# A Hymba decoder layer on one core: Silu gates, biases asked for a head ahead, memory tiles in the last group, value weights split between output products, and the cross norm in the exponential

## The chip, the cores and the metric

The kernel runs on one core of a Trainium2 chip, as one program in one launch. The metric is the device time of one execution in microseconds (us). The median of the runs is given, and beside it one execution recorded by the hardware profiler. TensorE (PE) multiplies; VectorE (DVE), ScalarE (ACT) and GpSimd (POOL) work on tiles in on-chip memory (SBUF) and in the accumulators (PSUM). SyncE (SP) asks for most transfers from device memory; ACT and POOL have queues of their own for a few.

## The reference

One layer with 512 tokens of width 1024: a half-weighted feed-forward, a mixer in which a state-space part (SSD, 16 heads in 4 groups) and 8 differential-attention heads share input and output projections, cross-attention into 256 memory tokens with 4 heads, and a second feed-forward. Cut to what the change touches:

```python
def swiglu(h, w_in, w_out):
    gate, up = jnp.split(h @ w_in, 2, axis=-1)
    return (jax.nn.silu(gate) * up) @ w_out

# differential attention: logits = q @ k * scale + bias[head], softmax, w = p0 - lam * p1

def memory_cross_attention(h, mem_n, w_cq, w_ck, w_cv, w_co):
    q = (h @ w_cq).reshape(bsz, seqlen, CROSS_HEADS, CROSS_HEAD_DIM)
    k = (mem_n @ w_ck).reshape(bsz, mlen, CROSS_HEADS, CROSS_HEAD_DIM)
    v = (mem_n @ w_cv).reshape(bsz, mlen, CROSS_HEADS, CROSS_HEAD_DIM)
    logits = jnp.einsum('bqhd,bkhd->bhqk', q, k) * (CROSS_HEAD_DIM ** -0.5)
    p = jax.nn.softmax(logits, axis=-1)
    ...

x = x + 0.5 * swiglu(rms_norm(x, norm_ffn1_w), ...)
x = x + hybrid_mixer(rms_norm(x, norm_mix_w), ...)
x = x + memory_cross_attention(rms_norm(x, norm_cross_w), rms_norm(mem, norm_mem_w), ...)
x = x + 0.5 * swiglu(rms_norm(x, norm_ffn2_w), ...)
```

## The kernel before

**Tiles and products.** Activations lie transposed: eight tiles `x[0..7]` of 128 channels x 512 tokens. Each float32 number is split into a high and a low half of the type that PE multiplies fast (`split_into`, line 152: ACT copies the high half, DVE subtracts it for the low one), and a product is three matmuls: high by high, high by low, low by high (`mm3`, line 312). A weight is loaded by SP into a raw buffer `wr` (six of them) and split into `wh` and `wl` (three of each; `load_w`, line 172), so a split waits until PE is done with the weight three before it. `proj` (line 318) runs over the eight input tiles: 24 matmuls of 128x512. The feed-forwards use larger Strassen-like blocks, `quad` (line 257), whose accumulators are called `qa`, `qb` and `qe`.

**Stages.** First feed-forward (0 to 358 us), memory keys and the norm of the mixer (to 384), attention heads and SSD groups (to 792), memory values (to 823), output product of the SSD part (to 868), cross-attention and its output product (to 987), second feed-forward and final norm.

**What sets the order.** `Order` (line 57) runs a list of dense generators one after another: `queries_keys`, `values`, `group_dense`, `out_attn`, `memory_values`, `out_proj` (added from line 1033 on). Each `yield` lets chains run that were spawned with `od.spawn(generator, after)`; a chain's step is due when the modelled time of the matmuls issued so far, `od.t`, has passed it. What a step issues enters the program there. The compiler's scheduler then orders PE, ACT and DVE; SP and POOL stay in program order. All engines work in order, so an instruction that waits holds up what stands behind it.

**The places of the change.** A gate of the feed-forward is `silu(g) * u`. `gated` (line 415) and `ffn_quads` (line 425) compute it as `tanh(g/2)` on ACT and `(tanh + 1) * g` on DVE, twice the Silu, which later factors take back. `queries_keys` (line 678) makes the queries `pq` and keys `pk` of a head and asks on ACT's queue for its tile `bias` of relative positions; `head` (line 689) adds the bias to the scores on DVE, exponentiates on ACT, and transposes the weights on PE (`pt`). In the SSD part `group_dense` (line 807) makes, for each group, two tiles by `xbc_tile` (line 794: a product `pxbc`, a convolution `conv` with one ACT and three DVE instructions that read its PSUM bank, and a Silu by `silu2`), two more of them, and two products `pz`. `group` (line 830) is a chain: transposes `pxt` and `pbt`, states `st`, decay rows `gate` and `th` that ACT's queue fetches from `cum_d`, then `y`, its square `ysq` on ACT, a sum on POOL, the matmul `pn`, and a row by two matmuls `nrow` (`row_of`, line 360). `out_attn` (line 773) is the attention's share of the output product (`pm`). Its last call, for outputs 5 to 7, loads its three weights at the start and spawns `memory_prep`: eight memory tiles `mem` through SP and eight splits `hm` on ACT and DVE. `memory_values` (line 985) multiplies the memory with eight weights `wcv` into four banks `pcv`. `Stat.finish` (line 388) makes a norm: eight `nps` matmuls over the sum of squares `nacc`, a small column by POOL, then two `nrow` matmuls and a copy for the row. `cross_dense` (line 1056) multiplies the queries of the cross-attention with this row; `cross` (line 1067) takes their scores and exponentials.

Of the kernel before, what the change touches and what calls it, by code (L numbers as in the profile page):

```python
# [14 lines left out]
ALU = mybir.AluOpType  # L15
# [85 lines left out]
def body(tc, a, dbg=None):  # L101
# [313 lines left out]
    def gated(pg, pu, row):  # L415
        gate = s2("gate")
        V.tensor_tensor(gate, pg, row, ALU.mult)
        th = s2("th")
        S.activation(th, gate, AF.Tanh, scale=0.5)
        V.scalar_tensor_tensor(gate, th, 1.0, gate, ALU.add, ALU.mult)  # L420
        if pu is not None:
            V.tensor_tensor(gate, pu, gate, ALU.mult)
        return gate

    def ffn_quads(xs, wq, st, nq, made, places, sums=None, fresh=False):

        for q in range(nq):
            for out in quad(xs, next(wq), next(sums) if sums else None, fresh and q == 0):
                if out is None:
                    yield  # L430
            gs, us = out
            gate, th = s4("gate"), s4("th")
            for i in range(2):
                row = st.row[:, None, i * H : (i + 1) * H].to_broadcast([P, 2, H])
                V.tensor_tensor(gate[:, 2 * i : 2 * i + 2], halves(gs[i]), row, ALU.mult)
            S.activation(th, gate, AF.Tanh, scale=0.5)
            V.scalar_tensor_tensor(gate, th, 1.0, gate, ALU.add, ALU.mult)
            for i in range(2):
                V.tensor_tensor(th[:, places[i]], halves(us[i]), gate[:, 2 * i : 2 * i + 2], ALU.mult)
            made(th)  # L440
            yield
# [42 lines left out]
    def ffn1(h, wa, on_final, at_out):  # L484
        row4, xs = None, []
        wq, plain = iter(a["f1q"]), a["f1i"]
        for ti, (_, nf) in enumerate(THIRDS):
            g = []
            nq = nf // 2
            if ti == 0:  # L490
# [6 lines left out]
                V.tensor_scalar(row4, st1.row, 0.25, None, ALU.mult)  # L497
# [179 lines left out]

    def queries_keys(hd):
        pq = acc("pq")
        yield from proj(pq, load_w(a["wq"][hd]), h)  # L680
        q = split("q", pq, -1.0)
        bias = s2("bias")
        S.dma_start(bias, bass.AP(rel_z.tensor, rel_z.offset + hd * P * (RW + 1) + P - 1, [[RW, P], [1, T]]))
        pk = acc("pk")
        yield from proj(pk, load_w(a["wk"][hd]), h)
        kq = split("k", pk)
        od.spawn(head(hd, q, kq, bias), W["h0"])
# [84 lines left out]

    def out_attn(hg, o0, o1, prep=False):
        if prep:
            od.spawn(memory_prep(hm2, 1.5), 4.0)
# [3 lines left out]
        for o in range(o0, o1):  # L779
            po = acc("pm")  # L780
            yield from proj(po, ws.get(o) or load_w(a["woa"][hg, o], 4 * P), heads)
            V.tensor_tensor(x[o], x[o], po, ALU.add)
        if o1 == KT:
            ya[4 * hg : 4 * hg + 4] = [None] * 4
# [22 lines left out]
    def group_dense(g):  # L807
        bc, xs, zs = [], [], []
        yield from xbc_tile(8 + g, bc)
# [175 lines left out]
    def memory_values():  # L985
# [5 lines left out]
        for k in range(KT - 2):  # L991
            w = load_w(a["wcv"][k])
# [31 lines left out]
    def upd_c(o, po):  # L1024
# [4 lines left out]
        if o == KT - 1:  # L1029
            h.clear()  # L1030
            od.spawn(st_c.finish(), 3.0)
# [24 lines left out]
    def cross_dense(hd):  # L1056
# [3 lines left out]
        q = []  # L1060
        for j in range(2):
            qf = s2("cqf")
            V.tensor_tensor(qf, ps[j], st_c.row, ALU.mult)
            q.append(split("cq", qf, 0.0625))
        od.spawn(cross(hd, q), W["c0"])

    def cross(hd, q):
        pth = [None, None]
        es = [None, None]
        for s in range(3):  # L1070
            if s < 2:
# [6 lines left out]
                V.tensor_reduce(mx, ps, axis=AX.X, op=ALU.max, negate=True)  # L1078
                sm = small("csm", 2)
                e = es[s] = s2("ce", shape=(P, 2, MEM))  # L1080
                for i in range(2):
                    S.activation(e[:, i], ps[:, i], AF.Exp, bias=mx[:, i : i + 1], accum_out=sm[:, i : i + 1])
# [184 lines left out]
    def ffn2():  # L1267
# [28 lines left out]
        for c, (_, nf) in enumerate(THIRDS2):  # L1296
            g = []
            yield from ffn_quads(xs_2, wq, st_2, nf // 2, block_tiles(g, nf // 2), BY_BLOCK, in_sums, c == 0)
            if c == 0:
                col4 = small("col4", 4, bufs=1)  # L1300
                ncol4 = small("ncol4", 4, bufs=1)
                V.tensor_scalar(col4, st_2.col, 0.25, None, ALU.mult)
                V.tensor_scalar(ncol4, st_2.col, -0.25, None, ALU.mult)
# [100 lines left out]
```

## Time and profile before

| | us |
|---|---|
| median of three runs (lowest to highest) | 1330.35 (1329.05 to 1330.5) |
| the profiled execution | 1330.79 |
| its span in the trace | 1329.0 |

The span is the time from the first to the last instruction in the trace; the rest of the profiled execution's time, 1.79 us, lies around it. A page of the profile gives each engine's busy time. A list of waits gives, for an engine, how long it stood idle before instructions of a kind and which instruction ended that. The chain of waits follows the last instruction back to what released it. A row of the timeline gives start and duration, engine, line, operation, output and inputs, and in brackets the idle time before it. In a group's row the numbers after the bar are the busy time in us, the mean in ns of one instruction, and the idle time of the engine before them.

### The profile page before, as it was taken

How to read it: one execution, taken by the hardware profiler on the slowest of the kernel's cores; microseconds unless marked ns; L12 is line 12 of the kernel's file. 1: busy time of each engine (PE TensorE's matmuls, PEld its weight loads, DVE VectorE, ACT ScalarE, POOL GpSimd, SP SyncE). 2: the span in 40 equal slices, each digit the busy share in tenths (PEclk: the TensorE clock that was granted, in tenths of full speed). 3: DMA queues.
4: the chain of work that ended last, by engine and by line, in shares of the span. 5: the costliest groups of instructions: out<-in, count | busy, mean ns of one | idle time of the engine just before them, and what ended most of it. 6: DMA issues, size and time to landing. Idle time of an engine off the chain costs nothing.

```text
span 1329.0 us, 20041 instructions
## 1 busy us (share of the span) xinstructions
PE 1307.0 (98%) x7769; PEld 1137.9 (86%) x7769; DVE 974.2 (73%) x1527; ACT 663.7 (50%) x1114; POOL 113.4 (9%) x127
## 2 busy tenths in 40 slices
PE   9999999999999999999999989999999999999997
PEld 7898998899887778777788878888889999989995
DVE  6874778487886486557867786656678878887886
ACT  6442445154454465336644655434465545554564
POOL 0000010000010111010112021020001100000001
PEclk9999999999999999999999999999999999999998
DMA  7335577555573724683365576775138975655662
GB/s 271 111 127 126 128 199 242 137 144 174 190 241 92 196 63 109 185 243 95 88 174 163 126 199 244 195 180 153 64 111 235 250 223 173 194 193 172 191 202 95
DMA packets 74143, 222.71 MB, mean 168 GB/s; under 512 B 8424, under 2 KB 20176, under 8 KB 73696
## 3 DMA queue, kind: packets, MB, share of 16 engines
q1 hardware_dynamic: 52400, 174.42, 38.3%
q0 software_dynamic: 11904, 40.45, 16.4%
q10 hardware_dynamic: 9744, 6.56, 2.4%
q8 instruction: 61, 1.00, 0.3%
q14 instruction: 34, 0.28, 0.1%
HBM read 219.24 MB, written 50.91 MB: 203 GB/s over the span
## 4 chain that ended last, share of the span: by engine, by line
PE 93%; DVE 2%; DMA 1%; ACT 1%; issue 1%; POOL 0%; POOLq 0%; SPq 0%; ACTq 0%; DVEq 0%
PE qb L240 12%; PE po L146 10%; PE pm L146 10%; PE qe L240 8%; PE qa L240 8%; PE pxbc L146 7%; PE pcq L146 3%; PE pz L146 3%; PE pv L146 3%; PE pq L146 3%; PE ob L1189 3%; PE pk L146 3%; PE oa L1189 2%; PE oe L1189 2%; PE pcv L146 2%; PE pa L146 2%
## 5 line engine op out<-in xcount | busy, mean ns | idle before, releaser
L155 ACT ACTIVATE wh<-wr 128x1024 fp32r<-128x1024 f32 (+2 forms) x311 | 316.9, 1021 | 366.7 <-PE po L146 61.8
L156 DVE TENSOR_TENSOR wl<-wr,wh 128x1024 fp32r<-128x1024 f32 (+2 forms) x311 | 365.5, 1177 | 110.4 <-ACT wh L155 108.2
L146 PE MATMUL po<-gh,wh 128*128 128x512 f32 x176 | 68.8, 392 | 0.0
L146 PE MATMUL po<-gl,wh 128*128 128x512 f32 x176 | 68.5, 390 | 0.0
L146 PE MATMUL po<-gh,wl 128*128 128x512 f32 x176 | 68.4, 389 | 0.0
L240 PE MATMUL qa<-hml,wh 128*128 128x256 f32 x216 | 61.1, 283 | 0.0
L240 PE MATMUL qa<-hmh,wl 128*128 128x256 f32 x216 | 61.1, 283 | 0.0
L240 PE MATMUL qa<-hmh,wh 128*128 128x256 f32 x216 | 61.1, 283 | 0.0
L146 PE MATMUL pxbc<-hnh,wh 128*128 128x512 f32 x128 | 52.2, 408 | 0.0
L705 ACT ACTIVATE ec<-ec,mn 128x512 f32<-128x512 f32 (+3 forms) x64 | 35.4, 555 | 32.4 <-DVE mn L704 32.4
L146 PE MATMUL pxbc<-hnh,wl 128*128 128x512 f32 x128 | 50.3, 393 | 0.0
L146 PE MATMUL pxbc<-hnl,wh 128*128 128x512 f32 x128 | 50.2, 392 | 0.0
L511 DVE TENSOR_TENSOR upd<-po,row 128x512 f32<-128x512 f32 x24 | 16.6, 690 | 39.2 <-PE po L146 39.0
L240 PE MATMUL qe<-s31h,wl 128*128 128x256 f32 x152 | 43.2, 284 | 0.5 <-DVE wl L156 0.5
L240 PE MATMUL qb<-s24h,wl 128*128 128x256 f32 x152 | 43.1, 284 | 0.5 <-DVE wl L156 0.5
L240 PE MATMUL qb<-s31h,wh 128*128 128x256 f32 x152 | 43.2, 284 | 0.0
L240 PE MATMUL qe<-s31h,wh 128*128 128x256 f32 x152 | 43.1, 284 | 0.0
L240 PE MATMUL qe<-s24h,wh 128*128 128x256 f32 x152 | 43.0, 283 | 0.0
L240 PE MATMUL qb<-hmh,wh 128*128 128x256 f32 x152 | 43.0, 283 | 0.0
L240 PE MATMUL qe<-s24h,wl 128*128 128x256 f32 x152 | 43.0, 283 | 0.0
L240 PE MATMUL qb<-hmh,wl 128*128 128x256 f32 x152 | 43.0, 283 | 0.0
L240 PE MATMUL qb<-hml,wh 128*128 128x256 f32 x152 | 43.0, 283 | 0.0
(443 smaller groups left out, 4064.6 us busy)
## 6 DMA issues: line engine op xcount, KB each, us to landing
wr<-in_f2q SPq DMA_DIRECT2D x44, 512.0 KB, 4.3
wr<-in_f1q SPq DMA_DIRECT2D x40, 512.0 KB, 4.0
isum<-in_f2q SPq DMA_DIRECT2D x22, 512.0 KB, 5.6
wr<-isum SPq DMA_DIRECT2D x22, 512.0 KB, 4.2
wsum<-in_f2b SPq DMA_DIRECT2D x20, 512.0 KB, 6.5
wr<-wsum SPq DMA_DIRECT2D x20, 512.0 KB, 4.6
wr<-in_f1q POOLq DMA_DIRECT2D x16, 512.0 KB, 6.3
wr<-in_f1o SPq DMA_DIRECT2D x16, 512.0 KB, 4.0
```

The source lines that it names most:

```text
L146: newest_mm[:] = [nc.tensor.matmul(out, w, x, start=start, stop=stop).ins]
L155: S.activation(hi, src, AF.Copy),
L156: V.tensor_tensor(lo, src, hi.bitcast(F32), ALU.subtract),
L240: newest_mm[:] = [nc.tensor.matmul(out, a_[:, wc], b_, start=first and f == 0 and kp == 0 and j == 0, stop=kp == n - 1 and j == 2, skip_gr ...
L511: V.tensor_tensor(upd, po, row4, ALU.mult)
L705: S.activation(ec[:, :n], ec[:, :n], AF.Exp, bias=mn, scale=-1.0, accum_out=sm[c][:, i : i + 1])
L1189: newest_mm[:] = [nc.tensor.matmul(ps, a_[:, ts], b_[:, ws], start=first and k == 0 and j == 0, stop=k == n - 1 and j == 2, skip_group_che ...
```

## The change

It has five parts. (1) The feed-forwards' gates become one ACT instruction, `Silu`, in place of `Tanh` and a DVE product, and factors of 0.25 become 0.5; an ACT_TABLE_LOAD is added ahead of the first Silu, of the first head's exponential and of the second feed-forward's first Silu. (2) `queries_keys` asks for the bias of the next head before its own products (the first one for its own too). (3) `memory_prep` is spawned at the start of the last `group_dense`, with its splits 3.0 apart in place of 1.5, and so its eight transfers stand on SP's queue behind the first weight of that group and ahead of all its others. (4) Two of the three last output products are each followed by the load and split of one value weight, and `memory_values` takes these two. (5) The norm ahead of the cross-attention stops after its column: the queries are split straight from PSUM, and the column scales the maximum and the exponential.

```diff
@@ -415,11 +415,8 @@
     def gated(pg, pu, row):
         gate = s2("gate")
         V.tensor_tensor(gate, pg, row, ALU.mult)
-        th = s2("th")
-        S.activation(th, gate, AF.Tanh, scale=0.5)
-        V.scalar_tensor_tensor(gate, th, 1.0, gate, ALU.add, ALU.mult)
-        if pu is not None:
-            V.tensor_tensor(gate, pu, gate, ALU.mult)
+        S.activation(gate, gate, AF.Silu)
+        V.tensor_tensor(gate, pu, gate, ALU.mult)
         return gate
 
     def ffn_quads(xs, wq, st, nq, made, places, sums=None, fresh=False):
@@ -433,8 +430,7 @@
             for i in range(2):
                 row = st.row[:, None, i * H : (i + 1) * H].to_broadcast([P, 2, H])
                 V.tensor_tensor(gate[:, 2 * i : 2 * i + 2], halves(gs[i]), row, ALU.mult)
-            S.activation(th, gate, AF.Tanh, scale=0.5)
-            V.scalar_tensor_tensor(gate, th, 1.0, gate, ALU.add, ALU.mult)
+            S.activation(gate, gate, AF.Silu)
             for i in range(2):
                 V.tensor_tensor(th[:, places[i]], halves(us[i]), gate[:, 2 * i : 2 * i + 2], ALU.mult)
             made(th)
@@ -494,7 +490,7 @@
                     else:
                         g.append(split("g", gated(*made, st1.row)))
                 row4 = s2("row4")
-                V.tensor_scalar(row4, st1.row, 0.25, None, ALU.mult)
+                V.tensor_scalar(row4, st1.row, 0.5, None, ALU.mult)
                 for n in range(NPLAIN - 2):
                     xs.append(block_sums(2 * n, C_FFN1, of_halves(h[2 * n], h[2 * n + 1])))
                     pg, pu = acc("pg"), acc("pu")
@@ -675,16 +671,24 @@
                 yield
         vs[hg] = [split("v", pv[tb]) for tb in range(4)]
 
+    biases = {}
+
+    def ask_bias(hd):
+        biases[hd] = s2("bias")
+        S.dma_start(biases[hd], bass.AP(rel_z.tensor, rel_z.offset + hd * P * (RW + 1) + P - 1, [[RW, P], [1, T]]))
+
     def queries_keys(hd):
+        if hd == 0:
+            ask_bias(0)
+        if hd < 7:
+            ask_bias(hd + 1)
         pq = acc("pq")
         yield from proj(pq, load_w(a["wq"][hd]), h)
         q = split("q", pq, -1.0)
-        bias = s2("bias")
-        S.dma_start(bias, bass.AP(rel_z.tensor, rel_z.offset + hd * P * (RW + 1) + P - 1, [[RW, P], [1, T]]))
         pk = acc("pk")
         yield from proj(pk, load_w(a["wk"][hd]), h)
         kq = split("k", pk)
-        od.spawn(head(hd, q, kq, bias), W["h0"])
+        od.spawn(head(hd, q, kq, biases.pop(hd)), W["h0"])
 
     def head(hd, q, kq, bias):
         es, w0, w1 = {}, {}, {}
@@ -770,9 +774,9 @@
         ya[hd] = split("ya", pt, wsub)
         dump(f"ya_{hd}", ya[hd][0])
 
+    wcv = []
+
     def out_attn(hg, o0, o1, prep=False):
-        if prep:
-            od.spawn(memory_prep(hm2, 1.5), 4.0)
         ws = {o: load_w(a["woa"][hg, o], 4 * P) for o in range(o0, o1) if prep}
         yield lambda: all(y is not None for y in ya[4 * hg : 4 * hg + 4])
         heads = ya[4 * hg : 4 * hg + 4]
@@ -780,6 +784,8 @@
             po = acc("pm")
             yield from proj(po, ws.get(o) or load_w(a["woa"][hg, o], 4 * P), heads)
             V.tensor_tensor(x[o], x[o], po, ALU.add)
+            if prep and len(wcv) < 2:
+                wcv.append(load_w(a["wcv"][len(wcv)]))
         if o1 == KT:
             ya[4 * hg : 4 * hg + 4] = [None] * 4
 
@@ -806,6 +812,8 @@
 
     def group_dense(g):
         bc, xs, zs = [], [], []
+        if g == 3:
+            od.spawn(memory_prep(hm2, 3.0), 1.0)
         yield from xbc_tile(8 + g, bc)
         yield from xbc_tile(12 + g, bc)
         for j in range(2):
@@ -989,7 +997,7 @@
 
         banks = [(tb, n) for tb in range(2) for n in range(2)]
         for k in range(KT - 2):
-            w = load_w(a["wcv"][k])
+            w = wcv[k] if k < len(wcv) else load_w(a["wcv"][k])
             for tb, n in banks:
                 part(k, w, tb, n)
                 yield
@@ -1028,7 +1036,7 @@
         dump(f"x2_{o}", x[o])
         if o == KT - 1:
             h.clear()
-            od.spawn(st_c.finish(), 3.0)
+            od.spawn(islice(st_c.finish(), 1), 3.0)
 
     hm, hm2 = [], []
     od.add(memory_keys())
@@ -1057,11 +1065,7 @@
         ps = [acc("pcq") for _ in range(2)]
         for j in range(2):
             yield from proj(ps[j], load_w(a["wcq"][2 * hd + j]), h_c)
-        q = []
-        for j in range(2):
-            qf = s2("cqf")
-            V.tensor_tensor(qf, ps[j], st_c.row, ALU.mult)
-            q.append(split("cq", qf, 0.0625))
+        q = [split("cq", ps[j], 0.0625) for j in range(2)]
         od.spawn(cross(hd, q), W["c0"])
 
     def cross(hd, q):
@@ -1076,10 +1080,12 @@
                         mm3(ps[:, i], q[j], ck[2 * hd + j], j == 0, j == 1, wc=qs)
                 mx = small("cmx", 2)
                 V.tensor_reduce(mx, ps, axis=AX.X, op=ALU.max, negate=True)
+                col = st_c.col[:, 2 * s : 2 * s + 2]
+                V.tensor_tensor(mx, mx, col, ALU.mult)
                 sm = small("csm", 2)
                 e = es[s] = s2("ce", shape=(P, 2, MEM))
                 for i in range(2):
-                    S.activation(e[:, i], ps[:, i], AF.Exp, bias=mx[:, i : i + 1], accum_out=sm[:, i : i + 1])
+                    S.activation(e[:, i], ps[:, i], AF.Exp, bias=mx[:, i : i + 1], scale=col[:, i : i + 1], accum_out=sm[:, i : i + 1])
                 rc = small("crc", 2)
                 V.reciprocal(rc, sm)
                 for i in range(2):
@@ -1299,8 +1305,8 @@
             if c == 0:
                 col4 = small("col4", 4, bufs=1)
                 ncol4 = small("ncol4", 4, bufs=1)
-                V.tensor_scalar(col4, st_2.col, 0.25, None, ALU.mult)
-                V.tensor_scalar(ncol4, st_2.col, -0.25, None, ALU.mult)
+                V.tensor_scalar(col4, st_2.col, 0.5, None, ALU.mult)
+                V.tensor_scalar(ncol4, st_2.col, -0.5, None, ALU.mult)
             at_end = c == len(THIRDS2) - 1
             if at_end:
                 for n in range(2):
```

Three places show how this moves instructions. The first is on ScalarE (ACT) around the last group's second `pxbc` product; `conv` reads the first product, and the `wh` behind it is the weight of the second. Before, in the last group (`wh_1529_7515` is the second product's weight):

```order
L799 ACTIVATE conv_1482_7313<-pxbc_1474_7270,par_77 128x512
L155 ACTIVATE wh_1515_7445<-wr_1514_7443 128x1024
L790 ACTIVATE th2_1483_7318<-conv_1482_7313 128x512
L155 ACTIVATE wh_1529_7515<-wr_1528_7513 128x1024
L155 ACTIVATE ysh_1493_7355<-y_1448_7101 128x512
L155 ACTIVATE ysh_1495_7360<-y_1463_7193 128x512
```

And of the change (`wh_1533_7517` is the second product's weight, `pxbc_1507_7422` the first product):

```order
L901 ACTIVATE gate_1441_7077<-gate_1441_7077,cum_240 128x128 x3
L159 ACTIVATE hm_1528_7494<-mem_1512_7437,par_77 128x256
L902 ACTIVATE gate_1441_7077<-gate_1441_7077 128x512
L805 ACTIVATE conv_1529_7506<-pxbc_1507_7422,par_77 128x512
L155 ACTIVATE wh_1533_7517<-wr_1532_7515 128x1024
```

The split of the second product's weight stood far ahead of the first product's end; now it stands behind the memory tiles' splits and behind the `conv` that reads that end. On TensorE of the change nothing stands between the two products:

```order
L146 MATMUL pxbc_1507_7422<-hnh_633_3850,wh_1509_7425 128x512
L146 MATMUL pxbc_1507_7422<-hnl_634_3851,wh_1509_7425 128x512
L146 MATMUL pxbc_1507_7422<-hnh_633_3850,wl_1510_7426 128x512
L146 MATMUL pxbc_1531_7514<-hnh_599_3680,wh_1533_7517 128x512
L146 MATMUL pxbc_1531_7514<-hnl_600_3681,wh_1533_7517 128x512
L146 MATMUL pxbc_1531_7514<-hnh_599_3680,wl_1534_7518 128x512
```

The second product's first matmul follows the first product's last, and its third needs `wl`.

The second place is on ACT in the last group's `pz` products, where the second group's `y` is squared (`ysq`). Before (the first 128x512 `wh` here is the first weight of the output products, `wh_1586_7819` the third):

```order
L921 ACTIVATE ysq_1551_7673<-y_1539_7584 128x512
L155 ACTIVATE wh_1580_7807<-wr_1579_7805 128x512
L921 ACTIVATE ysq_1552_7676<-y_1550_7669 128x512
L799 ACTIVATE conv_1553_7685<-pxbc_1544_7627,par_77 128x512
L155 ACTIVATE wh_1583_7813<-wr_1582_7811 128x512
L790 ACTIVATE th2_1554_7690<-conv_1553_7685 128x512
L790 ACTIVATE th2_1559_7725<-pz_1555_7693 128x512
L861 ACTIVATE btk_1577_7797<-pbt_1576_7793 128x384
L155 ACTIVATE wh_1586_7819<-wr_1585_7817 128x512
```

And of the change (`wh_1596_7839` is the third weight of the output products, `wh_1604_7868` the first value weight):

```order
L159 ACTIVATE hm_1556_7664<-mem_1517_7447,par_77 128x256
L929 ACTIVATE ysq_1560_7690<-y_1545_7592 128x512
L155 ACTIVATE wh_1596_7839<-wr_1595_7837 128x512
L929 ACTIVATE ysq_1561_7693<-y_1559_7686 128x512
L159 ACTIVATE hm_1562_7696<-mem_1518_7449,par_77 128x256
L805 ACTIVATE conv_1563_7705<-pxbc_1552_7641,par_77 128x512
L155 ACTIVATE wh_1604_7868<-wr_1603_7866 128x1024
```

The third weight, which takes the buffer of the last `pz` product's weight, moved from behind `conv` to between the two squares.

The third place is on VectorE (DVE) at the end of the first feed-forward, where the last output tiles are added and their squares summed in `nacc`. Before:

```order
L511 TENSOR_TENSOR upd_581_3594<-po_577_3569,row4_77_421 128x512
L512 TENSOR_TENSOR x7_107<-x7_107,upd_581_3594 128x512
L156 TENSOR_TENSOR wl_596_3674<-wr_594_3671,wh_595_3673 128x1024
L386 TENSOR_TENSOR nacc_534_3363<-nacc_534_3363,nsq_582_3597 128x512
L355 TENSOR_SCALAR nv_591_3648<-nps_590_3643 128x4
```

And of the change:

```order
L507 TENSOR_TENSOR upd_569_3543<-po_565_3518,row4_75_417 128x512
L156 TENSOR_TENSOR wl_583_3614<-wr_581_3611,wh_582_3613 128x1024
L508 TENSOR_TENSOR x6_103<-x6_103,upd_569_3543 128x512
L386 TENSOR_TENSOR nacc_528_3343<-nacc_528_3343,nsq_570_3546 128x512
L507 TENSOR_TENSOR upd_575_3574<-po_571_3549,row4_75_417 128x512
L508 TENSOR_TENSOR x7_107<-x7_107,upd_575_3574 128x512
L156 TENSOR_TENSOR wl_590_3654<-wr_588_3651,wh_589_3653 128x1024
L386 TENSOR_TENSOR nacc_528_3343<-nacc_528_3343,nsq_576_3577 128x512
```

In the tiles before the last one, a weight's low half `wl` moved from behind `x` to ahead of it; in the last tile the order is the same.

## The prediction

> **What bounds the kernel now.** I read three views in this order: the head of the page with its chain of waits, the list of what TensorE (PE) waits for, and the same span cut into windows.
>
> ```profile
> span 1329.0 us, 20041 instructions
> PE 1307.0 (98%) x7769; PEld 1137.9 (86%) x7769; DVE 974.2 (73%) x1527; ACT 663.7 (50%) x1114; POOL 113.4 (9%) x127
> PE 93%; DVE 2%; DMA 1%; ACT 1%; issue 1%; POOL 0%; POOLq 0%; SPq 0%; ACTq 0%; DVEq 0%
> ```
>
> PE is busy for 1307.0 of 1329.0 us and is 93% of the chain, so an edit counts only where it removes PE work, removes a PE wait, or makes a new one. Work taken from VectorE (DVE, 73%) or ScalarE (ACT, 50%) is worth nothing by itself.
>
> ```profile
> PE pcv L146 <- ACT wh L155: 3.8, 1, 3.8
> PE pt L150 <- DVE mn L704: 2.6, 1, 2.6
> PE qb L240 <- DVE wl L156: 0.5, 1, 0.5
> PE qe L240 <- DVE wl L156: 0.5, 1, 0.5
> ```
>
> In this list of waits (total, times, longest) two single waits stand out, and the change touches both. Each costs more than its idle time, as two pairs of windows show (columns: length, busy time and count of PE, weight loads, DVE, ACT, POOL, then the granted clock).
>
> ```profile
> 454.63:458.04 3.41, 0.79 (x4) 0.70 (x5) 3.05 (x9) 2.49 (x7) 0.00 (x0) 1.00 0.51 141
> 458.04:461.45 3.41, 3.41 (x10) 2.64 (x9) 2.73 (x10) 1.94 (x8) 0.00 (x0) 0.50 0.63 202
> 792.55:795.96 3.41, 0.15 (x1) 0.15 (x2) 2.94 (x7) 3.41 (x8) 0.00 (x0) 1.00 0.99 258
> 795.96:799.37 3.41, 3.26 (x8) 2.06 (x8) 3.41 (x5) 2.49 (x4) 0.00 (x0) 0.50 0.97 317
> ```
>
> A slice of 3.41 us in which PE was busy for 0.79 or 0.15 us is followed by one at clock 0.50. Half speed over 3.41 us loses 3.41/2 = 1.71 us of PE work. So a wait that empties most of one slice costs itself plus 1.71.
>
> **Biases a head ahead: -4.35.**
>
> ```profile
> 436.37 16.13 DMA bias<-rel_z
> L683 ACTq DMA_DIRECT2D bias<-rel_z x8: 326/338/355, 390.0 to 631.8; - x8
> 457.25 0.33 PE L150 MATMUL pt<-ident,ec 128*128 128x128 f32 x1 [2.64 <-DVE mn L704]
> ```
>
> The wait list blames DVE, but the chain of waits goes on to a bias transfer that took 16.13 us from its issue at 436.37; DVE's score rows were late behind it, and the transposes `pt` behind these. The eight biases are asked for from 390.0 to 631.8, 241.8/7 = 34.5 us apart; asked for one head earlier, the same transfer would land in the middle of the previous head's work. I take the whole wait and its slow slice: 2.64 + 1.71 = 4.35. If the transfer is as slow and lands late in its new place, nothing is gained.
>
> **Memory values: -5.90.**
>
> ```profile
> 794.71 1.04 ACT L155 ACTIVATE wh<-wr 128x1024 fp32r<-128x1024 f32 x1
> 795.81 1.11 PE L146 MATMUL pcv<-wh,hm 128*128 128x512 f32 x2 [3.79 <-ACT wh L155]
> 797.07 0.79 PE L146 MATMUL pcv<-wl,hm 128*128 128x512 f32 x1
> L156 DVE TENSOR_TENSOR wl<-wr,wh 128x1024 fp32r<-128x1024 f32 x280 | 342.3, 1224 | 104.8 <-ACT wh L155 103.4
> ```
>
> PE stands for 3.79 us before the first `pcv`, because the split of its weight starts on ACT only at 794.71. Two half-clock matmuls of about 0.43 us from 795.81 end at about 796.67, and the next starts at 797.07: 0.40 more, for the low half `wl`. With two value weights split between the last output products, PE should find both halves ready: 3.79 + 0.40 + 1.71 = 5.90. What takes the stall's place is below: the eight memory tiles now stand in the third group's work.
>
> **The third group's weight: +3.4, and +0.85 for the clock.** In the order before, ACT splits the weight of the group's second `pxbc` product ahead of `ysh`, long before it is needed:
>
> ```profile
> 732.66 1.06 ACT L155 ACTIVATE wh<-wr 128x1024 fp32r<-128x1024 f32 x1 [0.34 <-PE pz L146]
> 690.00:785.00 95.00, 95.00 (x498) 79.06 (x497) 72.09 (x111) 47.93 (x87) 14.94 (x14) 1.00 0.53 141
> L799 ACT ACTIVATE conv<-pxbc,par 128x512 f32<-128x512 f32 x16 | 12.2, 764 | 0.3 <-PE pxbc L146 0.3
> L802 DVE SCALAR_TENSOR_TENSOR conv<-pxbc,par,conv 128x511 f32<-128x511 f32 x16 | 11.9, 746 | 2.5 <-ACT conv L799 2.5
> 748.71 0.39 PE L146 MATMUL pxbc<-hnh,wl 128*128 128x512 f32 x1
> 748.93 0.39 PE L146 MATMUL pxbc<-hnh,wh 128*128 128x512 f32 x1
> ```
>
> PE has no idle time from 690 to 785. In the changed order that split stands on ACT behind a `conv` that reads the end of the first product, while PE goes straight on to the second. Matmuls start 0.23 us apart (748.71 to 748.93) but end after 0.39, so PE waits (0.39 - 0.23) + 0.76 + 1.06 = 2.0. Two matmuls later it needs `wl`, which DVE makes behind two taps of the convolution: 0.76 + 2 x 0.75 + 1.22 from the product's end, against 0.76 + 1.06 + 2 x 0.23: 1.2 more. The order alone thus gives 3.2; if ACT is late with the gate chain that stands ahead of `conv`, up to 4.1. I take 3.4, nearer the lower end since ACT is busy for 47.93 of 95 us there. The stall is cut by two matmuls of 0.45 us together, so a slice of 3.41 us can be as empty as 0.79 or not, by where its edge falls: 0 or 1.71, and I take half, 0.85.
>
> **The memory tiles, and y of the second group: +3.0.** Eight transfers and eight splits move 30 us ahead:
>
> ```profile
> 711.51 0.93 ACTq L827 DMA_DIRECT2D th<-cum_d  x2
> th<-cum_d ACTq DMA_DIRECT2D x8, 256.0 KB, 16.0
> SPq L946 <- DMA gate<-cum_d: 21.1, 2, 18.2
> 743.51 36.65 SPq L946 DMA_DIRECT2D mem<-in_memT  x8
> L159 ACT ACTIVATE hm<-mem,par 128x256 fp32r<-128x256 f32 x16 | 7.4, 494 | 0.0
> L160 DVE SCALAR_TENSOR_TENSOR hm<-mem,par,hm 128x256 fp32r<-128x256 f32 x16 | 7.2, 477 | 0.2 <-ACT hm L159 0.2
> L155 ACT ACTIVATE wh<-wr 128x512 fp32r<-128x512 f32 x23 | 14.4, 628 | 12.7 <-PE pm L146 4.6 <-PE oa L1189 1.9 <-PE qb L240 1.8
> L921 ACT ACTIVATE ysq<-y 128x512 f32<-128x512 f32 x8 | 5.0, 622 | 6.8 <-PE pm L146 4.8 <-DVE y L919 2.0
> L923 POOL TENSOR_TENSOR ysq<-ysq,ysq 128x512 f32<-128x512 f32 x4 | 6.6, 1662 | 153.4 <-ACT ysq L921 153.4
> 778.09 0.95 PE L146 MATMUL pn<-ones,ysq 128*128 128x1 f32 x8
> ```
>
> On SP's queue the eight issues took 36.65 us, because they wait for the decay rows `gate` and `th` that ACT's queue fetches (21.1 us of waits). Behind them stood value weights; now the weights of the second `pxbc` product and of all that follows in the group do. The rows they then wait for are those of the second group, the last asked for at 711.51 to 712.4; with a median of 16.0 from issue to landing SP is free at about 728.4. ACT, in its new order, wants the next weight at the end of the first product, 749: some 20 us of cover, so I cost the queue at nothing; a row that took all of these 20 us longer would stop PE at once.
>
> Of the splits, 8 x 0.494 on ACT and 8 x 0.477 on DVE find idle time where none stands in front of something PE waits for. At one place something late does. The third weight of the output products (128x512) is split between the two squares `ysq`, and its buffer comes free only at the last `pz` matmul; before, that split came behind `conv`. From that matmul's end: 0.39 + 0.63 + 0.62 + 1.66 (POOL's sum) = 3.3 until `pn` may start, while PE has eight `pm` and itself, 9 x 0.23 = 2.0: a wait of about 1.3. `conv` stands behind too, and holds the PSUM bank of the seventh output product: about 1.0. The row made of `pn` comes later by as much: up to 1.6. With the same path in the last group (0.9) and its successors the ceiling is 6. The floor is 0: before, `pn` at 778.09 did not wait. The waits share one lateness (a PE that stood once is late for the next), so I take half, 3.0.
>
> **The mix norm: +0.8.**
>
> ```profile
> 360.50 1.22 DVE L156 TENSOR_TENSOR wl<-wr,wh 128x1024 fp32r<-128x1024 f32 x1
> 361.64 0.68 DVE L386 TENSOR_TENSOR nacc<-nacc,nsq 128x512 f32<-128x512 f32 x1
> 362.56 0.95 PE L146 MATMUL nps<-ones,nacc 128*128 128x1 f32 x8
> ```
>
> `nps` starts 0.24 us after the last `nacc` ends. In the changed order DVE makes a `wl` ahead of `x` in each of the last tiles, so the sums run up to one `wl`, 1.22, later: 0 to 1.3, of which I take 0.8.
>
> **Cross norm: -0.5.**
>
> ```profile
> L146 PE MATMUL nrow<-ndiag,ones_r 128*128 128x512 f32 x16 | 6.1, 430 | 1.0 <-DVE ndiag L368 0.9
> ```
>
> Two of the sixteen `nrow` matmuls go, 2 x 0.23 = 0.45 at the start spacing, and a little of the 0.9 us of waits. The eight products with the row and the per-token column that replaces them are DVE work under PE's.
>
> **Silu: -0.5.**
>
> ```profile
> L437 DVE SCALAR_TENSOR_TENSOR gate<-th,gate 128x1024 f32<-128x1024 f32 x19 | 23.2, 1219 | 0.7 <-ACT th L436 0.6
> L340 ACT ACT_TABLE_LOAD x1 | 1.3, 1283 | 0.7 <-PEq L1394 0.7
> ```
>
> DVE loses 23.2 us and six smaller ones, all under PE's work; the two waits for `wl` of 0.5 us in the feed-forward (list above) may go: 0 to 1.0, taken at half. ACT gains three table loads, 3 x 1.28 = 3.9 us. They lie where the function changes, ahead of the first gate, the first head's exponential and the second feed-forward's gate; if the one before the exponential isn't hidden, it costs up to 1.3.
>
> The page "ScalarE: Activation LUTs" of the Trainium skill (What ACT_TABLE_LOAD costs) puts a switch at 1283 ns plus a drain of some 1380. The trace's one load agrees with the first figure, and no row shows the second; with both, three switches would be an estimated 8 us of ACT, and the worst case 2.7 in place of 1.3.
>
> **Sum**, against the profiled execution's own 1330.79 (1329.0 of span and 1.79 around it): 1330.79 - 4.35 - 5.90 + 3.4 + 0.85 + 3.0 + 0.8 - 0.5 - 0.5 = 1327.6. That run lies 0.44 above the median of the three, 1330.35, so I predict a median of **1327.2**.
>
> **Rivals.**
> *The repairs are given back in full.* The path of y takes its 6.0 and the slow slice falls: 1327.2 + 3.0 + 0.85 = 1331.0. For it: every term is forced by the order of ACT's instructions. Against: four waits in a row overlap. A variant is that the bias transfer is slow and late in its new place as well, 1327.2 + 4.35 = 1331.5; against it speaks that it then has the 34.5 us of a head more for its 16.13.
> *The third group falls behind (slower).* Eight splits of 0.494 on ACT and 0.477 on DVE enter a stretch in which DVE is busy for 72.09 of 95 us. If each stands ahead of something PE is about to need, they are worth 8 x 0.97 = 7.8 and the time is 1335.0. It decides from the point where PE's idle time between 740 and 830, 6.4 us in my sum, exceeds 12. Against it: ACT is idle half of the time.
> *The memory stall moves rather than goes*: the split of the third value weight is the new first late one, and pays its 3.79 again: 1331.0. Against it: eight `pcv` steps lie between.
>
> **How the numbers follow.** A measurement here can tell about 0.2%, 2.7 us, from no change: faster is under 1327.7, slower over 1333.0. My case, 0.46, has its own range of 1323 to 1328: stalls at their lower bounds give 1330.35 - 4.35 - 5.90 + 3.2 - 1.5 = 1321.8. The cases that end between 1327.7 and 1333.0 (waits in full, a late bias, a stall that moved) have 0.29; the third group behind, 0.25. With terms at both ends (1321.8 below, 1335.0 above) the range for 8 in 10 is 1323.0 to 1334.5.
>
> **What would show it.** Right: no `bias` in the chain of waits, no half-clock slice near 458 or 796, first `pcv` without a wait; ahead of the group's second `pxbc` a wait of 2 to 2.5 for `wh` and one of about 1.2 for `wl`; a wait of about 1 for `nps`; small ones at `pn` and `pm` near 780. Wrong: a bias transfer that lands after its scores, PE idle over 12 us between 740 and 830, more than one half-clock slice, or a wait of PE behind a table load.

## The result, and the profile after

The changed kernel takes 1329.57 us (median of 14 runs, 1326.96 to 1332.09), the kernel before in the same runs 1330.05 (14 runs, 1328.18 to 1330.91). The ratio is 0.9998 with a 95% interval of 0.9990 to 1.0006: no change that can be told from none. The range held; the likeliest case, 2.7 us or more faster, did not come. Three executions among all those of the experiments took 1.9 to 3.6 times as long as the others and are left out of the ratios.

The head of the page of the changed kernel (span; busy time, share and count by engine; shares of the chain of waits):

```profile
span 1328.6 us, 19969 instructions
PE 1307.6 (98%) x7767; PEld 1137.1 (86%) x7767; DVE 946.4 (71%) x1498; ACT 667.5 (50%) x1116; POOL 114.1 (9%) x127
PE 93%; DVE 3%; ACT 2%; issue 1%; POOL 1%; DMA 0%; POOLq 0%; SPq 0%; ACTq 0%; DVEq 0%
```

DVE is busy for 27.8 us less (23.4 of them by the Silu gates, by the trace of the run with these alone), the 1% of DMA in the chain (the bias) has become 0%, and PE is as busy as before. Of the list of PE's waits in the changed kernel, the lines that matter here:

```profile
PE pxbc L146 <- ACT wh L155: 1.8, 1, 1.8
PE nrow L146 <- POOL ndiag L368: 1.1, 1, 1.1
PE pm L146 <- DVE x L786: 0.9, 1, 0.9
PE pxbc L146 <- DVE wl L156: 0.8, 1, 0.8
PE pn L146 <- POOL ysq L931: 0.8, 2, 0.5
PE nps L146 <- DVE nacc L386: 0.3, 1, 0.3
```

The waits of 3.8 at `pcv` and 2.6 at `pt` have gone. In their place stand five entries in the last group (the one that the prediction calls the third, counted from 0): at the second `pxbc` product for both halves of its weight, and at `pn`, `pm` and `nrow`. All five places were named in the prediction; `nps` waits for 0.3 as before.

To see where the time went, the same matmul is looked up in both timelines (start in us; the last column is what the stretch since the row above gained or lost):

| start of | before | after | after - before | of this stretch |
|---|---|---|---|---|
| first `pq` | 384.31 | 384.15 | -0.16 | |
| `pq` of the fifth head | 576.91 | 572.22 | -4.69 | -4.5 bias |
| first `pxbc` of the last group | 740.77 | 736.06 | -4.71 | 0 |
| first `pf` behind the second `pxbc` | 755.06 | 756.29 | +1.23 | +5.9 the second product's weight |
| first `pcq` (cross-attention) | 868.63 | 870.11 | +1.48 | +0.3: 5.9 saved at `pcv`, 6.2 paid |
| first `qa` of the second feed-forward | 988.45 | 989.15 | +0.70 | -0.8 cross norm |
| last `ob` | 1319.12 | 1318.68 | -0.44 | -1.1 Silu |

So both repairs worked at their full size, and the last group gave them back. The largest loss is at the second `pxbc` product. Its rows in PE's timeline and ACT's, both of the changed kernel:

```profile
742.64 0.39 PE L146 MATMUL pxbc<-hnh,wl 128*128 128x512 f32 x1
744.84 0.51 PE L146 MATMUL pxbc<-hnh,wh 128*128 128x512 f32 x1 [1.81 <-ACT wh L155]
746.59 0.79 PE L146 MATMUL pxbc<-hnh,wl 128*128 128x512 f32 x1 [0.82 <-DVE wl L156]
```

```profile
743.06 0.78 ACT L805 ACTIVATE conv<-pxbc,par 128x512 f32<-128x512 f32 x1
743.74 1.99 ACT L155 ACTIVATE wh<-wr 128x1024 fp32r<-128x1024 f32 x2
```

ACT runs `conv` as soon as the first product ends, then the split, and PE waits behind both, as the order had it. What was underestimated is the clock (windows of the changed kernel, cut at the edges of its slow slices; columns as in the prediction; behind the clock stand DMA share and GB/s):

```profile
741.79:745.20 3.41, 1.60 (x8) 0.99 (x6) 2.71 (x5) 3.40 (x7) 0.00 (x0) 1.00 1.08 324
745.20:748.61 3.41, 2.59 (x7) 1.63 (x6) 3.41 (x5) 1.85 (x4) 0.00 (x0) 0.50 0.59 196
748.61:752.02 3.41, 3.41 (x10) 2.64 (x9) 2.32 (x4) 1.06 (x2) 0.00 (x0) 0.50 0.43 117
752.02:755.43 3.41, 3.41 (x17) 2.80 (x16) 0.07 (x1) 1.16 (x2) 0.00 (x0) 1.00 0.78 297
```

A slice with 1.60 us of PE work, near half, is followed by a half-clock slice; in that one PE waited once more (2.59 busy), and the next ran at half clock too. At half clock 2.59 + 3.41 us of busy time do the work of 3.0: another 3.0 lost beside the waits of 2.6. The last 0.3 of the 5.9 lies in matmuls that start late behind the waits.

### The profile page after: what moved, and what is told of

It reads as the page before. It is cut to its first block, busy times and chain, and to the rows that moved or that the text cites. A ratio compares the mean times of both kernels' runs of the same rounds, so it can differ in the third digit from the quotient of the medians.

```text
span 1328.6 us, 19969 instructions
## 1 busy us (share of the span) xinstructions
PE 1307.6 (98%) x7767; PEld 1137.1 (86%) x7767; DVE 946.4 (71%) x1498; ACT 667.5 (50%) x1116; POOL 114.1 (9%) x127
## 4 chain that ended last, share of the span: by engine, by line
PE 93%; DVE 3%; ACT 2%; issue 1%; POOL 1%; DMA 0%; POOLq 0%; SPq 0%; ACTq 0%; DVEq 0%
PE qb L240 12%; PE po L146 10%; PE pm L146 9%; PE qe L240 8%; PE qa L240 8%; PE pxbc L146 7%; PE pk L146 3%; PE pq L146 3%; PE pcq L146 3%; PE pv L146 3%; PE pz L146 3%; PE ob L1195 3%; PE oa L1195 2%; PE oe L1195 2%; PE pa L146 2%; PE pg L146 2%
## 5 line engine op out<-in xcount | busy, mean ns | idle before, releaser
L240 PE MATMUL qb<-s31h,wl 128*128 128x256 f32 x152 | 43.0, 283 | 0.0
```

Of the source, the lines that this page charges most:

```text
L240: newest_mm[:] = [nc.tensor.matmul(out, a_[:, wc], b_, start=first and f == 0 and kp == 0 and j == 0, stop=kp == n - 1 and j == 2, skip_gr ...
```

## The experiments

Twelve runs, in four jobs of one chip each. A difference in us is the ratio's distance from 1 times the median of the kernel before in that job, with the interval's ends. Each kernel below is made from the kernel before or from the changed one.

**Each part alone.** The bias alone, on the kernel before (shortened to the place of asking):

```diff
     def queries_keys(hd):
+        if hd == 0:
+            ask_bias(0)
+        if hd < 7:
+            ask_bias(hd + 1)
```

> The kernel before with one part of the change: each head asks for the bias of the next. Theory A (the change's parts add up, and the two traces laid over each other give each part's size): 4.5 us less than before, near 1325.6, no wait at pt near 455 and no half-clock slice there. Rival B (the slow bias transfer of the traced execution was an accident that most executions do not have): less than 1.5 us of gain.

Measured: 1326.55 against 1329.27, ratio 0.9978 (0.9969 to 0.9987), 2.9 us less (1.7 to 4.1). The wait at `pt` and its slow slice are gone. The gain lies between the two theories, and other traces say why. The same transfer in the run of the memory parts, which leave the bias alone: the landing times of all eight (min, median, max), and the DVE row that waits for the late one:

```profile
DMA to landing us min/median/max: 2.6/3.9/12.2
```

```profile
449.00 0.69 DVE L704 CUSTOM_DVE_ANT_0 ec<-ps,bias 128x512 f32<-128x512 f32 x1 [3.68 <-DMA bias<-rel_z]
```

Here it took 12.2 us, DVE waited, and PE's list shows no wait at `pt`. In the trace of the cross norm alone it took 15.0, and PE waited for this long:

```profile
PE pt L150 <- DVE mn L704: 1.7, 1, 1.7
```

With 14.3 (Silu alone) the wait at `pt` was 1.0, with 16.1 (before) it was 2.6 and a slow slice. In all five traces that ask for the bias at its old place, the second head's transfer is the slow one. The time from the first `pq` to the fifth head's, a stretch that the other parts leave alone, follows it:

| trace | transfer landed after | stretch | half-clock slices in it |
|---|---|---|---|
| memory parts alone | 12.2 | 188.5 | 0 |
| Silu alone | 14.3 | 190.7 | 0 |
| cross norm alone | 15.0 | 191.4 | 0 |
| value weights alone (below) | 16.0 | 193.6 | 2 |
| kernel before | 16.1 | 192.6 | 1 |

With the bias asked for a head earlier the stretch is 188.1 to 188.2 in all nine traces. So the transfer costs from 0.4 us at 12.2 to 4.5 and 5.4 at 16; the execution that was profiled first was among the dear ones.

**The memory parts alone** (the spawn of `memory_prep` in `group_dense(3)`, and the two value weights between the output products):

> The kernel before with the two memory parts alone: memory tiles at the start of the last group, two value weights split between the last output products. Theory A (these parts remove 5.9 us at the value products and pay about 12 in the last group, 5.9 of them at its second pxbc product with two slices at half clock, 6.2 on the path of y and in a finer interleaving): 6 us more than before, near 1336. Rival C (the stall at the second pxbc product comes from the Silu gates' other order, and the memory parts keep their gain): 5.9 less, near 1324.

Measured: 1333.09 against 1329.27, ratio 1.0035 (1.0023 to 1.0047), 4.7 us more (3.1 to 6.2). The waits of 1.8 and 0.9 at `pxbc` and 0.5, 0.9 and 1.1 at `pn`, `pm` and `nrow` are all there without the Silu gates, whose other order is thus no cause, and rival C is out; theory A's 6 lie in the interval.

**Silu alone, and the cross norm alone:**

> The kernel before with the Silu gates alone. Theory A (it shortens the lateness of weights in the two feed-forwards): 1.5 us less, near 1328.5, of which about 1.1 in the second feed-forward; the matmuls nps of the mix norm wait for 0.3 or less. Rival D (VectorE's work lies wholly under TensorE's, and three table loads are hidden too): within 0.5 of before.

> The kernel before with the cross norm's column in the exponential alone. Theory A (two nrow matmuls and their wait go): 0.9 us less, near 1329.2. Rival: the queries split straight from PSUM free their banks no earlier and the products of the column delay the exponentials: 0 or up to 1 us more.

Measured: Silu 0.9994 (0.9983 to 1.0005), 0.8 us less (2.3 less to 0.7 more); cross norm 1.0006 (0.9995 to 1.0017), 0.8 more (0.7 less to 2.3 more). Neither is told from zero by its times. The 0.9 less of theory A for the cross norm lies just outside its interval. By their traces, Silu gains 1.1 in the second feed-forward against the first trace of the kernel before (0.9 against the four other traces with the old gates), and the cross norm 0.7 between the first `pcq` and the first `qa`. But in both traces the wait at `pcv` is followed by two half-clock slices and not by one, and the stretch from there to `pcq` is 0.7 and 1.2 longer than before. A gain of 1 us is as large as this chance.

**All parts but the memory's:**

> The change without its two memory parts: biases a head ahead, Silu gates, the cross norm's column. Theory A (the memory parts together cost what the other three gain): 4 to 5 us less than before, the sum of 2.9 (biases alone), 0.8 (Silu alone) and 0.9 (the cross norm's step in its trace); the wait of 3.8 us at the first pcv is still there. Rival E (the three parts overlap or lengthen each other, as the measured plus 0.8 of the cross norm alone suggests): 2 to 3 us less.

Measured: 1324.38 against 1329.04, ratio 0.9966 (0.9954 to 0.9979), 4.5 us less (2.8 to 6.1), as theory A had it; the wait of 3.8 at `pcv` is there. So the memory parts cost the changed kernel about what the rest gains.

**The two value weights alone**, on the kernel before (shortened; `memory_values` takes them as in the change):

```diff
             V.tensor_tensor(x[o], x[o], po, ALU.add)
+            if prep and len(wcv) < 2:
+                wcv.append(load_w(a["wcv"][len(wcv)]))
```

> The kernel before with two value weights split between the last output products, and the memory tiles at their old place. Theory F (the value weights' stall comes from SP's queue, where they stand behind eight memory tiles that take 37 us, so splitting them early doesn't help unless the tiles go first): the wait for the split at pcv stays at 2 us or more, and the time is at most 2 us under before. Rival (the place of the split on ScalarE alone made the stall): the wait at pcv is gone, and the time is 4 to 7.5 us less.

Measured: 1325.84 against 1329.04, ratio 0.9975 (0.9965 to 0.9985), 3.3 us less (2.0 to 4.7). Theory F falls by its time (at most 2 us) and holds by its row: PE still waits for 2.0, but now for a memory tile's split.

```profile
PE pcv L146 <- ACT hm L159: 2.0, 1, 2.0
```

And that wait is cheap, since the slices it falls into stay full enough (windows of this run, at the edges of the clock's slices):

```profile
790.83:794.24 3.41, 2.20 (x10) 1.50 (x8) 2.57 (x5) 3.36 (x11) 0.00 (x0) 1.00 1.06 261
794.24:797.66 3.42, 2.59 (x11) 2.17 (x12) 2.54 (x5) 3.42 (x9) 0.00 (x0) 1.00 1.04 246
```

The wait is cut by a slice's edge: PE is busy for 2.20 and 2.59 us in the two slices, and the clock stays at 1.00. More than half of the prize at `pcv` was to be had without moving the tiles.

**The tiles alone** (the change without these value weights):

> The change without the split of two value weights between the output products: tiles at the start of the last group, value weights asked for by the value products themselves. Theory G2 (the tiles bring the stall at the second pxbc product and the waits at pn and pm; the early value weights bring the whole gain at pcv): both pxbc waits and those at pn (0.5) and pm (0.9) stay, a wait of 2 us or more at pcv is back, and the time is 2 to 5 us over the change's, near 1333. Rival (the tiles alone remove most of the wait at pcv): the wait there is under 1 us and the time is within 1 us of the change's.

Measured: 1329.46 against 1327.50, ratio 1.0018 (1.0009 to 1.0027), 2.4 us more (1.2 to 3.6); its absolute time is that of the changed kernel. The waits came as theory G2 had them except the one at `pcv`:

```profile
PE pxbc L146 <- ACT wh L155: 1.8, 1, 1.8
PE pcv L146 <- DVE wl L156: 1.4, 1, 1.4
PE pm L146 <- DVE x L784: 0.9, 1, 0.9
```

1.4 in place of 2 or more, and the time that theory G2 gave did not come either. Beside the run of the value weights alone: either memory part alone removes half or more of the wait of 3.8 at `pcv`. What the early value weights add to the tiles can't be told from the times: the changed kernel ran on other chips, and after `pxbc` it had two slow slices in one trace and one in another, while this run's trace has one. The traces say more: from the first `pf` to the first `pcq` this run takes 114.1 us and the changed kernel 113.8 in both of its traces. Beside the early tiles, the value weights are worth about 0.3 us.

**The tiles later, and in between** (the edit of the later one; in the other, the spawn stands between the two products):

```diff
-        if g == 3:
-            od.spawn(memory_prep(hm2, 3.0), 1.0)
         yield from xbc_tile(8 + g, bc)
         yield from xbc_tile(12 + g, bc)
+        if g == 3:
+            od.spawn(memory_prep(hm2, 2.0), 1.0)
```

> The change with the memory tiles asked for after the last group's second pxbc product instead of ahead of its first, 2.0 apart. Theory G (what the change pays in the last group comes from the tiles standing ahead of the second product's weight on SP's queue, which moves its split behind the convolution): the waits of 1.8 and 0.8 us at pxbc and both half-clock slices near 746 go, which is 5.9 us, and the time is 5 to 8 us under before, near 1323. Rival H (ScalarE and VectorE are too full in the last group for eight splits more, wherever they enter): the waits appear at another product of that group, and the time stays within 2 us of the change's.

> The same with the memory tiles asked for between the last group's two first pxbc products: behind the second product's weight is not reached, but the third's and fourth's are. Theory G: the stall moves from the second product to the third and is smaller (0.2 to 1 us for each half of the weight), the time is 3 to 6 us under before. Rival H: within 2 us of the change's.

Measured against 1329.04: late 1321.87, ratio 0.9948 (0.9935 to 0.9960), 6.9 us less (5.3 to 8.6); between 1323.44, ratio 0.9961 (0.9947 to 0.9974), 5.2 less (3.5 to 7.0). With the tiles late no wait at `pxbc` is left, none of the new ones at `pn`, `pm` and `nrow`, nor any half-clock slice from 400 to 860 us; the longest new wait is this:

```profile
PE pst L146 <- DVE xde L861: 0.9, 1, 0.9
```

With the tiles between, the stall moved on to the third product, 0.3 and 0.5 for its two halves, and the longest new wait is one of 1.8 at `pxt`. Rival H falls: eight splits do fit into the group. **The late version beats both kernels.**

**Only the weight moved.** In the changed kernel, the second product's weight is asked for ahead of the tiles, whose time stays (shortened; `xbc_tile` takes the weight that it is given):

```diff
+        w0 = load_w(a["wxbc"][8 + g])
+        w1 = load_w(a["wxbc"][12 + g]) if g == 3 else None
         if g == 3:
             od.spawn(memory_prep(hm2, 3.0), 1.0)
-        yield from xbc_tile(8 + g, bc)
-        yield from xbc_tile(12 + g, bc)
+        yield from xbc_tile(8 + g, bc, w0)
+        yield from xbc_tile(12 + g, bc, w1)
```

> The change with one thing moved: in the last group the weight of the second pxbc product is asked for ahead of the eight memory tiles and not behind them; the tiles keep their time. Theory G1 (only that weight's place behind the tiles made the stall at the second product, since its split is then ordered behind the convolution): the waits of 1.8 and 0.8 us at pxbc and both half-clock slices near 746 go, and the waits at pn, pm and nrow near 780 to 796 (0.5, 0.9, 1.1) stay: about 5.9 us less than the change, near 1323.5. Rival H (the tiles' splits on ScalarE and VectorE made it): the second product still waits for 1 us or more, and the time is within 3 us of the change's.

Measured: 1324.34 against 1327.50, ratio 0.9977 (0.9967 to 0.9986). That is 5.2 us less than the changed kernel had taken, but only 3.1 (1.9 to 4.4) under the kernel before, which was itself faster in this job. So the pair was run once more together.

> The changed kernel itself once more, beside the kernel with the weight moved first, on one chip: 1328 to 1331, both traces alike up to the last group. It shows the two waits at pxbc again; whether one slice or two run at half clock after them is open (theory: one or two by the place of the stall in the slices, 1.7 us apart).

> The kernel with the second product's weight asked for ahead of the tiles, again, on one chip with the change: theory G1 says 5 to 6 us less than the change in the same job; the ratio to the kernel before differs between chips with how late that kernel's bias transfer lands (2.9 us in the middle, 0 to 4.5).

Measured in one job: the change 1328.79 (ratio 1.0009, 1.0000 to 1.0018), the weight first 1324.24 (0.9969, 0.9958 to 0.9979), 4.55 us less than the change by the medians and 5.3 by the two ratios. The waits at `pxbc` are gone, those behind them stayed to the tenth:

```profile
PE nrow L146 <- POOL ndiag L368: 1.1, 1, 1.1
PE pm L146 <- DVE x L786: 0.9, 1, 0.9
PE pn L146 <- POOL ysq L933: 0.8, 2, 0.5
```

Theory G1 holds, at about the lower end of its size, and the windows of the changed kernel in this job show why:

```profile
739.96:743.37 3.41, 2.33 (x11) 1.60 (x9) 2.51 (x6) 3.40 (x9) 0.00 (x0) 1.00 1.05 316
743.37:746.78 3.41, 1.65 (x6) 1.08 (x7) 3.38 (x5) 1.85 (x3) 0.00 (x0) 1.00 0.62 205
746.78:750.19 3.41, 3.41 (x10) 2.64 (x9) 3.41 (x5) 2.16 (x4) 0.00 (x0) 0.50 0.59 172
```

The same two waits, 1.8 and 1.0, lie differently against the slices here. The first begins in one that stays busy for 2.33; its rest and the whole second wait fall into the next, busy for 1.65, which is followed by the slow one. That one was full, and the clock came back after a single slice. By the start times of this job's two traces the stretch cost 5.1 us, against 5.9 with two slices.

The cause lies in the order that was fixed ahead of time, and not in a late transfer. In the changed kernel SP's rows are:

```profile
692.63 29.07 SPq L954 DMA_DIRECT2D mem<-in_memT  x8
722.34 1.01 SPq L174 DMA_DIRECT2D wr<-in_wxbc  x2
```

The first of these two is the second product's weight. Its time to landing:

```profile
DMA to landing us min/median/max: 7.5/7.5/7.5
```

The weight was asked for at 722.34, so it landed at 729.9 and lay there for 13.9 us until ACT split it at 743.74. With the tiles ahead of it in the program, its split had been put behind `conv` in ACT's order, and ACT kept to that. Why the scheduler chose this order, the runs do not show.

## Why the prediction was right or wrong, step by step

**The whole: the range held, partly by luck.** The sum gave 3.2 us less for the traced execution, and the two traces differ by 0.4. Two terms were too small by 4.9 together (the third group's weight and the path of y), and the others were too pessimistic by 2.1 together; these partly cancel. Of the signs of being wrong, one came: more than one half-clock slice.

**What bounds the kernel, and the places of the new waits: right.** PE's chain was the measure, both old waits went, and the five new entries of PE's list stand where the prediction had them; 0.27 at `py` came besides.

**Memory values, -5.90: right in size** in the first pair of traces (no wait at the first `pcv`, no slow slice).

**Biases, -4.35: right for that pair (-4.5), too large for the median.** The step took the price from one execution, whose transfer of 16.13 us was the slowest of five; by the times it is 2.9.

**The third group's weight, +3.4 and +0.85: the waits right, the clock wrong.** The waits came to 1.81 and 0.82, 2.6 against 3.2. The clock term was "0 or 1.71, and I take half". The four traces with this stall show one slow slice in two of them (1.7) and two in the others (3.0 in the changed kernel), never none. The step that failed is the reading of a slice as empty only at about 0.79 us of work: 1.60 and 1.65 were enough. With starts behind the waits the whole is 5.0 to 6.0 in these traces, in place of 4.25. The page "TensorE: Matmul & The Clock Gate" of the Trainium skill (What's actually happening) lets the rate fall after at least one idle window of about 3.4 us. Here the slices have that length, but one with 1.65 of 3.41 us of work was enough, so in this case far less idleness than a whole window lowered the rate.

**The path of y, +3.0: the waits right, the term too small.** The first wait came by the steps that the prediction gave, as ACT's, POOL's and PE's rows of the changed kernel show. The third weight's split waits for the last `pz` matmul, the second square stands behind it, then come POOL's sum and `pn`:

```profile
781.85 0.63 ACT L155 ACTIVATE wh<-wr 128x512 fp32r<-128x512 f32 x1 [2.25 <-PE pz L146]
782.38 0.62 ACT L929 ACTIVATE ysq<-y 128x512 f32<-128x512 f32 x1
783.08 1.28 POOL L931 TENSOR_TENSOR ysq<-ysq,ysq 128x512 f32<-128x512 f32 x1 [56.10 <-ACT ysq L929]
784.41 1.05 PE L146 MATMUL pn<-ones,ysq 128*128 128x1 f32 x8 [0.53 <-POOL ysq L931]
```

It came to 0.53 in place of 1.3, mostly since POOL's sum took 1.28 and not 1.66 and the split started 0.2 after the matmul's start and not 0.39. The sum "0 to 6, I take half" rested on waits that share one lateness. Those that the list and the timeline name, 0.53 and 0.23 at `pn`, 0.86 at `pm`, 1.09 at `nrow` and 0.27 at `py`, make 3.0 just so. But the stretch paid 6.2. The other 3.2 has no releaser in the lists. Adding up the steps from one matmul's start to the next in the two traces divides it: the steps into these waits take 1.0 us more than the idle time itself, and about 2.2 lies in steps without any wait. There the order is finer: the kind of matmul changes 42 times in place of 34 (the 16 `py` of a half group come as 2 and 14, with value products between), and the second 512-wide matmul behind a few small ones starts after 0.31 to 0.34 in place of 0.23. The prediction put this at nothing. The waits come with the early tiles: the tiles alone bring 0.5 at `pn` and 0.9 at `pm`, moving the weight leaves all of them, and with the tiles late none is there.

**The mix norm, +0.8: wrong, 0.** The one wait for `nps` of 0.3 is in both lists, and the first `pq` starts 0.16 us earlier than before: no delay by the `wl` moved ahead of `x` shows.

**Cross norm -0.5 and Silu -0.5:** -0.8 and -1.1 in the first pair of traces, the second a little over its bound of 0 to 1.0; the times of each alone can't tell them from zero. No wait of PE's stands behind one of the three table loads. The first exponential's, in ACT's timeline of the changed kernel:

```profile
398.95 0.59 ACT L608 ACTIVATE dtf<-pdt 32x512 f32<-32x512 f32 x1 [1.74 <-PE pdt L146]
399.55 1.28 ACT L709 ACT_TABLE_LOAD   x1
400.85 0.72 ACT L709 ACTIVATE ec<-ec,mn 128x512 f32<-128x512 f32 x1
```

The load starts within 0.02 us of the end of the instruction ahead of it, and the next one starts within 0.02 us of the load's end. The page "ScalarE: Activation LUTs" of the Trainium skill (What ACT_TABLE_LOAD costs) counts a drain of some 1.38 us more for a switch; here the 1.28 agree, and there is no room for the drain.

**The rivals.** The one that came true is that the repairs are given back in full, priced at 1331.0 (measured 1329.57), for the two reasons that it named: the path of y in full and the slow slices. That the third group falls behind is excluded: its condition, over 12 us of idle PE between 740 and 830, did not come (5.6), and in the run with the tiles late the same splits fit. That the memory stall only moves is excluded too: the changed kernel's list has no such wait at `pcv`.

## What to carry to other kernels

In these traces, a wait that empties half of a 3.41 us slice costs its length and 1.7 us more, and up to twice that when the next slice is broken too: count slices, not waits, and look where a planned stall falls. When loads are moved ahead in a queue, look for the loads that they displace, and where their first users now stand in the order: here a split came 13.9 us after its data had landed. And a stall behind one slow transfer has a price that varies from run to run; take it from several executions before setting it against certain costs.

## What the runs showed that was not expected

With each trace divided at the edges that its own clock shows, the bound is sharp. In all fourteen, between 20 and 1300 us, every slice at full clock in which PE was busy for 1.65 us or less was followed by one at half clock, and none that was busy for 1.71 or more was. This is the nearest one above, in the run of the cross norm alone:

```profile
452.60:456.01 3.41, 1.71 (x12) 1.04 (x10) 2.36 (x9) 2.51 (x6) 0.00 (x0) 1.00 0.54 152
456.01:459.42 3.41, 3.37 (x19) 2.58 (x19) 3.34 (x11) 1.93 (x7) 0.00 (x0) 1.00 0.49 138
```

So about half of a slice decides, and a wait of 1.7 us there cost no slow slice. The way back asks for more: a slice at half clock that was busy for 2.68 us or less was followed by another, and only those busy for 3.26 or more by full clock.

The landing time of one and the same bias transfer, in traces whose eight take a median of 3.3 to 3.9, ran from 12.2 to 16.1 us. Asked for a head earlier, the slowest of the eight took 22.1 in the changed kernel, and no engine's wait for a bias is left in its trace.
